# The normed recurrent outputs split into halves during attention, the softmax-merge DMAs on POOL's queue, and the rwkv output weights laid out by block

## The chip, the cores and the metric

The kernel runs on one NeuronCore of a Trainium2 chip. The metric is the device time of one execution in microseconds; the kernel before takes 1726.71 us, the median of 3 runs (1720.41 to 1730.13). The core has a matmul engine (TensorE, PE in the profile; its weight loads are PEld), a vector engine (VectorE, DVE), an activation engine (ScalarE, ACT), GpSimd (POOL) and SyncE (SP). SP computes nothing and issues DMAs; ACT and POOL issue DMAs too, each on a queue of its own, in the order of that engine's instructions. All matrix work on PE runs in a 32-bit form whose products are made exact enough by splitting each factor into a high and a low half (hi, lo) and adding three products, hi·hi, hi·lo and lo·hi. The high half is a rounded copy on ACT, the low half a subtraction on DVE.

## The reference, cut to what matters

```python
h = rms_norm(x, norm1_gain)
p = h @ w_in
q, k, v, p_rwkv, p_gate = jnp.split(p, [...], axis=-1)
...
for g, (win, dil) in enumerate(ATT_PATTERNS):     # 3 groups of 4 heads, dilation 1, 4, 16
    o_g, l_g = dilated_window_attention(q[:, :, g], k[:, :, g], v[:, :, g], ..., win, dil)
...
wts = jax.nn.softmax(jnp.stack(lses, axis=0), axis=0)          # over the 3 groups
att = jnp.einsum('gbsh,gbshe->bshe', wts, jnp.stack(outs, axis=0))
y_att = att.reshape(B, S, ATT_OUT_WIDTH) @ w_att_out           # 256 -> 1024
y_rwkv = rwkv7_time_mix(p_rwkv, ...)                           # ends in o @ w_rwkv_out, 512 -> 1024
gates = jax.nn.sigmoid(p_gate)
mixed = gates[..., :D] * y_att + gates[..., D:] * y_rwkv
x = x + mixed @ w_out
x = x + hierarchical_moe(rms_norm(x, norm2_gain), ...)         # 32 experts, top 2 of a group
```

S = 1024 tokens, D = 1024, everything in fp32.

## The kernel before, in words

Activations lie transposed: a tile holds 128 channels on the partitions and the 1024 tokens along the free axis. The program runs, in this order: the input projection, its gate columns being kept as filler work; the rwkv chunk scan, whose normed outputs go to a DRAM scratch dON (4 tiles of 128 x 1024); attention; a mixing stage; the out-projection with the router; and the 32 experts.

**Attention** runs six units (3 groups x 2 pairs of heads) of eight blocks each. Between the blocks, `fill` emits matmuls of the gate columns; their tanh goes to the scratch dGA from POOL's queue, 128 x 512 at a time. At the end of a unit, `finish` writes the unnormalized output Og to the scratch dOG and the row maxima and sums to dML.

**The mixing stage** is what the change edits. Before, it does the following.

- It loads dON, splits it into ohi and olo (line 1111 for the loads, 1087 and 1088 for the hi and lo half of every `split`), and loads the eight small tiles MLc from dML, from ACT's queue (line 1116).
- From MLc it makes the weights of the softmax over the three groups (wgt, lines 1118 to 1127), stores them to dWG (ACT's queue, line 1129), and reads them back later as broadcasts over 64 partitions (wb, named raw<-dWG, ACT's queue, line 1192).
- The rwkv projection: for eight blocks n of 128 output channels and two halves h of the tokens, 12 matmuls (`mm3`, line 1096) into one PSUM tile pa, of which there are three. The weight block wr comes from SP (line 1137) and is split into wrh and wrl. DVE multiplies the result with the gate and stores it in mix (line 1178). At the same time the blocks of w_out are loaded (line 1182) and split into woh and wol, 16 pairs of 128 x 512.
- The merge: for each of the two pairs of heads, three dOG tiles are multiplied with their broadcasts (line 1193, the third on POOL) and added (1197); the sum is split into ahi and alo.
- The attention projection: w_att_out has two blocks (line 1204), each split into hi and lo; 16 PSUM tiles of 6 matmuls; DVE multiplies with the gate (1219), and DVE or POOL adds to mix (1220).
- The out-projection starts with the splits of mix by 128 tokens (mxh), made in the pool pmx.

**What sets the order.** The kernel is written with a tile framework: every engine gets its own list of instructions, and a scheduler puts them in order by the order of the code and by priorities (`high_priority`; a negative offset defers). A tile pool hands out buffers; a tile whose buffer was used before waits for the last reader of the earlier one. A pool that is opened after another was closed may take its memory, and then its first writer waits for the readers of what lay there. An engine runs its list strictly in order, so a DMA that an engine issues waits in that list like any other instruction. DMAs also share a small set of completion semaphores in turn, so that an issue can wait for an earlier transfer on the same semaphore. In the mixing stage all this is decided by the scheduler.

**The junction** to the out-projection: ACT's list holds six small DMA issues there (lines 1345 to 1361: a gain row, the router's weights and biases, constants rc, and a zero fill of an output strip, zpad). In the expert weights' prefetch, SP loads the first expert matrices into tiles that come free (line 1326).

Of the kernel before, what the change touches and what calls it, by code (L numbers as in the profile page):

```python
# [34 lines left out]
NRAW2 = 5  # L35
# [76 lines left out]
def host_layout(inp):  # L112
# [70 lines left out]
def block_kernel(ctx, tc, I, out, dbg=None):  # L183
# [697 lines left out]

    s3 = ExitStack()
# [34 lines left out]
    def prelude(u):  # L917
# [46 lines left out]
        u.Og = p4.tile([128, S], F32, name="Og")  # L964
# [115 lines left out]
    s9 = ctx.enter_context(ExitStack())  # L1080
    mr = s9.enter_context(tc.tile_pool(name="mr", bufs=NRAW, reuse_waits="tile"))
# [3 lines left out]

    def split(hi, lo, raw):
        nc.scalar.activation(hi, raw, AF.Copy)
        nc.vector.tensor_tensor(lo, raw, hi.bitcast(F32), op=ALU.subtract)
# [11 lines left out]
    pmx = s9.enter_context(tc.tile_pool(name="pmx", bufs=2, reuse_waits="tile"))  # L1100
    s6 = ExitStack()
    pf = s6.enter_context(tc.tile_pool(name="pf", bufs=1, reuse_waits="tile"))
    ohi = pf.tile([128, 4, S], F32R, name="ohi")
    olo = pf.tile([128, 4, S], F32R, name="olo")
    ahi = pf.tile([128, 2, S], F32R, name="ahi")
    alo = pf.tile([128, 2, S], F32R, name="alo")
    s7 = ExitStack()
    p7 = s7.enter_context(tc.tile_pool(name="p7", bufs=2, reuse_waits="tile"))
    for p in range(4):
        raw = raw4k()  # L1110
        nc.sync.dma_start(raw, dON[p])
        split(ohi[:, p], olo[:, p], raw)
    ML = p7.tile([128, 2, 3, 32], F32, name="MLc", bufs=1)
    for a in range(2):
        for h in range(4):
            nc.scalar.dma_start(ML[32 * h:32 * h + 32, a], dML[a, h].rearrange("g (b t) -> b g t", t=32))
    mm_ = p7.tile([128, 32], F32, name="mmin", bufs=1)
    nc.vector.tensor_tensor(mm_, ML[:, 0, 0], ML[:, 0, 1], op=ALU.min)
    nc.vector.tensor_tensor(mm_, mm_, ML[:, 0, 2], op=ALU.min)
    wg = p7.tile([128, 3, 32], F32, name="wgt", bufs=1)  # L1120
# [4 lines left out]
    nc.vector.tensor_tensor(mm_, mm_, ML[:, 1, 2], op=ALU.add)
    nc.vector.reciprocal(mm_, mm_)
    nc.vector.tensor_tensor(wg, wg, mm_[:, None, :].to_broadcast([128, 3, 32]), op=ALU.mult)
    for h in range(4):
        nc.scalar.dma_start(dWG[h].rearrange("g (b t) -> b g t", t=32), wg[32 * h:32 * h + 32])

    wav = I["w_att_out"].rearrange("(k p) n -> p k n", p=128)
    wrv = I["w_rwkv_out"].rearrange("(k p) n -> p k n", p=128)
    wrs = {}

    def load_wr(n):
        wr = p7.tile([128, 4, 128], F32, name="wr")
        nc.sync.dma_start(wr, wrv[:, :, 128 * n:128 * n + 128])
# [5 lines left out]
    load_wr(0)  # L1143
    load_wr(1)
# [562 lines left out]
```

## Time and profile before

| | |
|---|---|
| median of 3 runs | 1726.71 us (1720.41 to 1730.13) |
| profiled execution | 1720.78 us |
| its span in the profile | 1719.0 us |
| mean granted TensorE clock | 0.981 |
| PE busy | 1644.6 us, 96% of the span |
| DVE busy | 1194.2 us |
| ACT busy | 871.3 us |
| POOL busy | 287.3 us |
| DMA traffic | 363.44 MB, mean 211 GB/s |

The stages in the trace of that execution, in us from the start of the span: attention to about 890, its last gate matmul at 899; the rwkv projection from 904 to 961; the attention projection from 962 to 987; the out-projection and the router to 1104; the experts to the end. A row of a timeline has the start, the duration, the engine, the line, the operation, output and inputs, shapes and how many were merged, and in brackets the idle time of the engine just before it and what ended it. PE's matmuls overlap, so the distance of two starts is the pace, not the duration of a row. PEclk is the granted clock as a share of full speed. The DMA share is the mean busy share of the core's 16 DMA engines.

### The profile page before, as it was taken

What the parts mean: (1) busy time and instruction counts of PE and PEld (TensorE: products, weight loads), DVE (VectorE), ACT (ScalarE), POOL (GpSimd) and SP (SyncE); (2) the same over time, 40 slices, a digit from 0 to 9 for tenths busy, and PEclk for the clock granted to TensorE, in tenths of its full rate; (3) what the DMA queues carried; (4) which work ended last, traced back from release to release, by engine and by line L of the source; (5) the groups of instructions that cost most, each with busy time, mean ns of one, the idle gap of its engine ahead of it and who ended that gap; (6) DMA issues with size and microseconds to landing.
All of it is one profiled execution on the core that took longest, in us unless ns stands there. A gap on an engine that the chain in (4) does not pass through costs nothing. (4 is left out here: it accounts for less than half of the span.)

```text
span 1719.0 us, 25855 instructions
## 1 busy us (share of the span) xinstructions
PE 1644.6 (96%) x9395; PEld 1308.6 (76%) x9396; DVE 1194.2 (69%) x2181; ACT 871.3 (51%) x1315; POOL 287.3 (17%) x314
## 2 busy tenths in 40 slices
PE   8999998999999999999998899789999999999996
PEld 6677777777777777777766677678888888888884
DVE  5648798784552444434336756689999999998985
ACT  4524444423221333344343122378888888887774
POOL 0100103133430000000100221212221222211211
PEclk9999999999999999999998999889999999999998
DMA  8324324476642111111249783679999999999994
GB/s 297 130 80 137 116 87 153 141 239 195 210 138 73 37 44 37 45 41 53 88 149 269 213 298 134 239 255 376 382 374 365 375 371 374 363 363 354 373 373 119
DMA packets 145619, 363.44 MB, mean 211 GB/s; under 512 B 17316, under 2 KB 62772, under 8 KB 145484
## 3 DMA queue, kind: packets, MB, share of 16 engines
q1 hardware_dynamic: 123108, 303.67, 49.1%
q0 software_dynamic: 15872, 50.35, 10.5%
q10 hardware_dynamic: 6504, 7.69, 1.7%
q8 instruction: 76, 1.25, 0.3%
q14 instruction: 59, 0.48, 0.1%
HBM read 307.49 MB, written 62.29 MB: 215 GB/s over the span
## 5 line engine op out<-in xcount | busy, mean ns | idle before, releaser
L1536 PE MATMUL pb<-u,xTh 128*128 128x512 f32 x1024 | 338.2, 406 | 0.5 <-ACT xTh L1531 0.5
L307 PE MATMUL pa<-xhi,wh 128*128 128x512 f32 x736 | 300.3, 408 | 2.9 <-DVE qT L905 1.4
L307 PE MATMUL pa<-xlo,wh 128*128 128x512 f32 x736 | 302.0, 410 | 0.0
L307 PE MATMUL pa<-xhi,wl 128*128 128x512 f32 x736 | 298.2, 406 | 2.4 <-DVE wl L278 2.4
L1422 DVE TENSOR_TENSOR u<-raw,u 128x1024 fp32r<-128x1024 f32 x216 | 254.7, 1219 | 18.0 <-ACT u L1421 15.9
L1421 ACT ACTIVATE u<-raw 128x1024 fp32r<-128x1024 f32 x216 | 223.6, 1056 | 30.6 <-PE pb L1536 19.0
L1536 PEld LDWEIGHTS pb<-u,xTh 128*128 128x128 f32 x1024 | 191.1, 189 | 40.3 <-ACT xTh L1531 1.2
L1536 PE MATMUL pb<-u,xTl 128*128 128x512 f32 x512 | 207.5, 405 | 0.0
L307 PEld LDWEIGHTS pa<-xhi,wh 128*128 128x128 f32 x736 | 140.3, 191 | 35.9 <-DVE qT L905 1.7
L307 PEld LDWEIGHTS pa<-xhi,wl 128*128 128x128 f32 x736 | 140.3, 191 | 34.9 <-DVE wl L278 3.2
L307 PEld LDWEIGHTS pa<-xlo,wh 128*128 128x128 f32 x736 | 140.4, 191 | 34.6 <-issue 4.0
L1422 DVE TENSOR_TENSOR u<-mix,u 128x1024 fp32r<-128x1024 f32 x128 | 151.4, 1219 | 11.2 <-ACT u L1421 10.0
L1536 PE MATMUL pa<-u,hTh 128*128 128x512 f32 x512 | 143.4, 401 | 0.9 <-ACT hTh L1531 0.9
L1421 ACT ACTIVATE u<-mix 128x1024 fp32r<-128x1024 f32 x128 | 133.2, 1057 | 16.6 <-PE pb L1536 9.6
L980 DVE SCALAR_TENSOR_TENSOR Sb<-pb,rqk,bias 128x128 f32<-128x128 f32 (+1 forms) x96 | 35.5, 408 | 126.7 <-PE pb L979 119.0
L1515 POOL DMA_INDIRECT out<-row,tba x30 | 78.8, 2628 | 202.1 <-ACT u L1421 171.5
L1536 PEld LDWEIGHTS pa<-u,hTh 128*128 128x128 f32 x512 | 93.5, 188 | 22.4 <-ACT hTh L1531 1.5
L1536 PEld LDWEIGHTS pb<-u,xTl 128*128 128x128 f32 x512 | 96.8, 189 | 17.6 <-DVE xTl L1532 0.2
L276 ACT ACTIVATE wh<-wr 128x1024 fp32r<-128x1024 f32 x49 | 51.8, 1056 | 107.3 <-PE pa L307 88.6
L1536 PE MATMUL pa<-u,hTl 128*128 128x512 f32 x256 | 80.7, 396 | 1.2 <-DVE hTl L1532 1.2
L1509 POOL DMA_INDIRECT xin<-dH,tbl x32 | 38.2, 1194 | 250.8 <-PE pb L1530 248.0
L984 ACT ACTIVATE Sb<-Sb,ML 128x128 f32<-128x128 f32 (+1 forms) x96 | 42.3, 442 | 54.5 <-DVE ML L982 54.5
(415 smaller groups left out, 2823.8 us busy)
## 6 DMA issues: line engine op xcount, KB each, us to landing
raw<-in_w_expert_up SPq DMA_DIRECT2D x72, 512.0 KB, 11.8
raw<-in_w_expert_gate SPq DMA_DIRECT2D x71, 512.0 KB, 5.3
raw<-in_w_expert_down SPq DMA_DIRECT2D x71, 512.0 KB, 12.2
wr<-in_w_in SPq DMA_DIRECT2D x49, 512.0 KB, 3.5
mix<-in_w_expert_down SPq DMA_DIRECT2D x46, 512.0 KB, 13.0
mix<-in_w_expert_gate SPq DMA_DIRECT2D x42, 512.0 KB, 5.0
mix<-in_w_expert_up SPq DMA_DIRECT2D x40, 512.0 KB, 11.9
dGA<-gs POOLq DMA_DIRECT2D x32, 256.0 KB, 2.9
```

The lines of the kernel that those rows point to most:

```text
L276: nc.scalar.activation(wh, wr, AF.Copy)
L307: nc.tensor.matmul(ps, a[:, k, :], b[:, k, hs], start=(n == 0), stop=(n == 23))
L980: nc.vector.scalar_tensor_tensor(Sb[:, hh, 0:nk], pS[:, 0:nk], u.rn[:, 0, i, hh:hh + 1], u.bias[:, hh, 256 - nk:], op0=ALU.mult, op1=ALU.add)
L984: nc.scalar.activation(Sb[:, hh, 0:nk], Sb[:, hh, 0:nk], AF.Exp, bias=u.ML[:, i, hh:hh + 1], accum_out=u.ML[:, i, 2 + hh:3 + hh])
L1421: nc.scalar.activation(hi, raw, AF.Copy)
L1422: nc.vector.tensor_tensor(lo, raw, hi.bitcast(F32), op=ALU.subtract)
L1509: nc.gpsimd.indirect_dma_start(out=dst, out_offset=None, in_=src, in_offset=bass.IndirectOffsetOnAxis(ap=idx, axis=0), bounds_check=S - 1, ...
L1515: nc.gpsimd.indirect_dma_start(out=out, out_offset=bass.IndirectOffsetOnAxis(ap=idx, axis=0), in_=src, in_offset=None, compute_op=ALU.add)
L1536: nc.tensor.matmul(ps, x, w, start=first, stop=last)
```

## The change

1. The halves ohi and olo get eight tiles of their own in a pool `pf` that is opened before attention. A generator `on_steps` loads dON from POOL's queue and splits it, one step per attention block, from the second unit on. For the room, Og goes from two buffers to one, Sb from three to two, and mt takes a slot that other tiles of attention share.
2. The last unit's writes to dOG and dML go out on POOL's queue, and so do the loads of MLc, the stores of dWG, the loads of dOG and the broadcasts wb. The third product of the merge moves from POOL to DVE. The steps that make the weights are a generator that is advanced inside the loop over n, the last two of them with a negative priority offset.
3. w_rwkv_out is laid out on the host as 8 blocks, so that a load of a block reads 2 KB runs; the first two loads get priority. Gates are loaded as full rows (128 x 1024) instead of halves.
4. The eight slots of `pf` serve afterwards as gate tiles (fs), as places for the expert prefetch and for the low halves of the first two splits of mix. Raw tiles `mr` and the pool of ahi and alo close with the mixing stage, and pmx is opened after that.

```diff
+    s9 = ctx.enter_context(ExitStack())
+    pf = s9.enter_context(tc.tile_pool(name="pf", bufs=1, reuse_waits="tile"))
+    ohi = [pf.tile([128, S], F32R, name=f"ohi{p}") for p in range(4)]
+    olo = [pf.tile([128, S], F32R, name=f"olo{p}") for p in range(4)]
...
+    def on_steps():
+        for p in range(4):
+            yield
+            raw = p4.tile([128, S], F32, tag="sq", name="raw")
+            nc.gpsimd.dma_start(raw, dON[p])
+            yield
+            split(ohi[p], olo[p], raw)
...
-        u.Og = p4.tile([128, S], F32, name="Og")
+        u.Og = p4.tile([128, S], F32, name="Og", bufs=1)
...
-        Sb = p4.tile([128, 2, 256], F32, name="Sb", bufs=3)
+        Sb = p4.tile([128, 2, 256], F32, name="Sb", bufs=2)
...
-        nc.sync.dma_start(dOG[2 * u.g + u.hp], u.Og)
+        q = nc.gpsimd if u is units[-1] else nc.sync
+        q.dma_start(dOG[2 * u.g + u.hp], u.Og)
         for hh in range(2):
-            nc.sync.dma_start(dML[:, 2 * u.hp + hh, u.g], mt[hh:4:2])
+            q.dma_start(dML[:, 2 * u.hp + hh, u.g], mt[hh:4:2])
...
             fill(FA)
+            if n > 0:
+                next(ons, None)
...
-    pmx = s9.enter_context(tc.tile_pool(name="pmx", bufs=2, reuse_waits="tile"))
-    s6 = ExitStack()
...
-            nc.scalar.dma_start(ML[32 * h:32 * h + 32, a], dML[a, h].rearrange("g (b t) -> b g t", t=32))
+                nc.gpsimd.dma_start(ML[32 * h:32 * h + 32, a], dML[a, h].rearrange("g (b t) -> b g t", t=32))
...
-        nc.scalar.dma_start(dWG[h].rearrange("g (b t) -> b g t", t=32), wg[32 * h:32 * h + 32])
+            nc.gpsimd.dma_start(dWG[h].rearrange("g (b t) -> b g t", t=32), wg[32 * h:32 * h + 32])
...
-        nc.sync.dma_start(wr, wrv[:, :, 128 * n:128 * n + 128])
+        nc.sync.dma_start(wr, I["w_rwkv_out"][n])
...
-    load_wr(0)
-    load_wr(1)
+    with tc.high_priority(offset=600):
+        load_wr(0)
+        load_wr(1)
...
+        if n in (0, 2, 3):
+            with tc.high_priority(offset=-400 if n else 0):
+                next(mw, None)
...
-            nc.sync.dma_start(og, dOG[2 * g + hp])
+            nc.gpsimd.dma_start(og, dOG[2 * g + hp])
             wb = raw4k()
             for hh in range(2):
-                nc.scalar.dma_start(wb[hrs[hh]], dWG[2 * hp + hh, g:g + 1].to_broadcast([64, S]))
-            (nc.gpsimd if g == 2 else nc.vector).tensor_tensor(og, og, wb, op=ALU.mult)
+                nc.gpsimd.dma_start(wb[hrs[hh]], dWG[2 * hp + hh, g:g + 1].to_broadcast([64, S]))
+            nc.vector.tensor_tensor(og, og, wb, op=ALU.mult)
...
     s7.close()
     s6.close()
+    pmx = s9.enter_context(tc.tile_pool(name="pmx", bufs=2, reuse_waits="tile"))
...
-            ml = raw4k().bitcast(F32R).rearrange("q (n t) -> q n t", t=128)
+            ml = fslot(7 - i).bitcast(F32R).rearrange("q (n t) -> q n t", t=128)
```

The order of instructions moves at three places that matter below. A row has the line, the operation, output and inputs, the shape, and how many follow one another. The first place is ACT's list from the end of the last attention unit (Og, mt) into the rwkv projection. Before:

```order
L1012 ACTIVATE Og<-pb 128x8x64
L1026 ACTIVATE mt<-pb 4x8x64 x2
L383 ACTIVATE gs<-gs 128x512
L1087 ACTIVATE ohi<-raw 128x1024 x4
L1116 DMA MLc<-dML 32x3x32 x8
L1087 ACTIVATE wrh<-wr 128x512
L1122 ACTIVATE wgt<-wgt 128x96
L1087 ACTIVATE wrh<-wr 128x512
```

With the change:

```order
L1035 ACTIVATE Og<-pb 128x8x64
L1049 ACTIVATE mt<-pb 4x8x64 x2
L385 ACTIVATE gs<-gs 128x512
L894 ACTIVATE wrh<-wr 128x512
L385 ACTIVATE gs<-gs 128x512
L894 ACTIVATE wrh<-wr 128x512
L1139 ACTIVATE wgt<-wgt 128x96
```

The four copies ohi and the eight loads MLc no longer stand between the last evacuations of attention and the first wrh.

The second place is POOL's list from the last unit's writes to the last broadcast. Before, POOL had the dGA stores, two products of the merge and additions to mix there, and no load. With the change:

```order
L1054 DMA dOG<-Og 128x1024
L1056 DMA dML<-mt 2x1024 x2
L386 DMA dGA<-gs 128x512
L1132 DMA MLc<-dML 32x3x32 x8
L386 DMA dGA<-gs 128x512
L1214 DMA raw<-dOG 128x1024
L1147 DMA dWG<-wgt 32x3x32 x4
L1217 DMA raw<-dWG 64x1024 x2
L1214 DMA raw<-dOG 128x1024
L1217 DMA raw<-dWG 64x1024 x2
```

The pair of the last two rows comes six times in all. All of the merge's transfers now stand in one list.

The third place is ACT's list at the junction to the out-projection. Before:

```order
L1087 ACTIVATE raw<-raw 128x1024
L1087 ACTIVATE mxh<-mix 128x1024 x2
L1345 DMA g_8582<-in_g 128x1024
L1347 DMA wr_8584<-in_w_rt 128x8x36
L1349 DMA g2c<-in_g2c 128x8
L1352 DMA br_8589<-in_b_rt 128x36
L1354 DMA rc<-in_rc 128x208
L1361 DMA out<-zpad 1024x1x128
L1472 ACTIVATE pa,ss_8620<-xt 128x512
```

With the change:

```order
L894 ACTIVATE raw<-raw 128x1024
L1368 DMA g_8572<-in_g 128x1024
L1370 DMA wr_8574<-in_w_rt 128x8x36
L1372 DMA g2c<-in_g2c 128x8
L1375 DMA br_8579<-in_b_rt 128x36
L1377 DMA rc<-in_rc 128x208
L1384 DMA out<-zpad 1024x1x128
L894 ACTIVATE mxh<-mix 128x1024 x2
L1495 ACTIVATE pa,ss_8606<-xt 128x512
```

The copies mxh have moved behind the six DMA issues.

More of the change, by code (lines that the diff above doesn't have):

```diff
@@ L34 @@
 NRAW = 6
-NRAW2 = 5
+NRAW2 = 3
+NS8 = 8
 BHT = 2
@@ L143, in host_layout @@
     f["bucket1h"], f["relmask"] = host_bucket()
-    for k in ("w_att_out", "w_rwkv_out", "w_out"):
+    for k in ("w_att_out", "w_out"):
         f[k] = inp[k][0]
+    f["w_rwkv_out"] = inp["w_rwkv_out"][0].reshape(4, 128, 8, 128).transpose(2, 1, 0, 3)
     f["g2c"] = inp["norm2_gain"][0].reshape(8, 128).T
@@ L879, in block_kernel, with fslot, split @@
     sT.close()
+    s9 = ctx.enter_context(ExitStack())
+    pf = s9.enter_context(tc.tile_pool(name="pf", bufs=1, reuse_waits="tile"))
+    ohi = [pf.tile([128, S], F32R, name=f"ohi{p}") for p in range(4)]
+    olo = [pf.tile([128, S], F32R, name=f"olo{p}") for p in range(4)]
+    ftags = [f"ohi{p}" for p in range(4)] + [f"olo{p}" for p in range(4)]
+    def fslot(j):
+        return pf.tile([128, S], F32, tag=ftags[j], name="fs")
+    def split(hi, lo, raw):
+        nc.scalar.activation(hi, raw, AF.Copy)
+        nc.vector.tensor_tensor(lo, raw, hi.bitcast(F32), op=ALU.subtract)
+    def on_steps():
[5 more added lines that the diff above has]
+            split(ohi[p], olo[p], raw)
     s3 = ExitStack()
@@ L1097, in mm3 @@
                 i += 1
-    pmx = s9.enter_context(tc.tile_pool(name="pmx", bufs=2, reuse_waits="tile"))
-    s6 = ExitStack()
[L1102 to L1106, printed above, removed]
+    pa_ = s6.enter_context(tc.tile_pool(name="pa_", bufs=1, reuse_waits="tile"))
+    ahi = pa_.tile([128, 2, S], F32R, name="ahi")
@@ L1107, in block_kernel @@
+    alo = pa_.tile([128, 2, S], F32R, name="alo")
     s7 = ExitStack()
     p7 = s7.enter_context(tc.tile_pool(name="p7", bufs=2, reuse_waits="tile"))
[L1109 to L1114, printed above, removed]
-        for h in range(4):
-            nc.scalar.dma_start(ML[32 * h:32 * h + 32, a], dML[a, h].rearrange("g (b t) -> b g t", t=32))
@@ L1170, in block_kernel @@
     wov = I["w_out"].rearrange("(k p) n -> p k n", p=128)
+    mw = merge_weights()
+    ga1 = gate(1, 0)
     for n in range(8):
         wh, wl = wrs.pop(n)
+        ga = ga1
+        if n + 1 < 8:
+            ga1 = gate(1, n + 1)
         for h in range(2):
             hs = slice(512 * h, 512 * h + 512)
-            ga = gate(1, n, h)
             ps = psA.tile([128, 512], F32, name="pa")
-            mm3(ps, [((wh[:, k], wl[:, k]), (ohi[:, k, hs], olo[:, k, hs])) for k in range(4)])
-            nc.vector.scalar_tensor_tensor(mixv(n, h), q4(ga), 1.0, q4(ps), op0=ALU.add, op1=ALU.mult)
+            mm3(ps, [((wh[:, k], wl[:, k]), (ohi[k][:, hs], olo[k][:, hs])) for k in range(4)])
+            nc.vector.scalar_tensor_tensor(mixv(n, h), q4(ga[:, hs]), 1.0, q4(ps), op0=ALU.add, op1=ALU.mult)
         if n + 2 < 8:
@@ L1206, in block_kernel @@
         split(wa[k][0], wa[k][1], raw[k])
-    gas = []
-    for tag in ("ohi", "olo"):
-        t = pf.tile([128, 8, 512], F32, tag=tag, name=tag + "g")
-        gas += [t[:, j] for j in range(8)]
+    gas = [gate(0, n) for n in range(2)]
+    gas += [gate(0, 2 + j, fslot(j)) for j in range(6)]
     for h in range(2):
@@ L1292, in block_kernel @@
     mr2 = s9.enter_context(tc.tile_pool(name="mr2", bufs=NRAW2, reuse_waits="tile"))
[L1293 removed]
+    areas = ["mr2"] * NRAW2 + [("s", j) for j in range(NS8)] + list(range(8)) + ["mx"] * 2 + ["ph"] * NPH
     NR = len(areas)
@@ L1461, in block_kernel @@
             if c == 1 and i < 7:
-                load_raw(N0 + NRAW2 + NRAW + i)
+                load_raw(N0 + NRAW2 + NS8 + i)
                 load_x(i + 1)
                 if i == 1:
-                    for j in range(NRAW):
+                    for j in range(NS8):
                         load_raw(N0 + NRAW2 + j)
```

56 lines of the change are left out of this document (28 added, 28 removed).

## The prediction, made before the result was known

> **What bounds the kernel now.** I read the page first, then the waits of TensorE, then the windows around those waits, and only then the timelines of PE, ACT and SP in them.
>
> ```profile
> span 1719.0 us, 25855 instructions
> PE 1644.6 (96%) x9395; PEld 1308.6 (76%) x9396; DVE 1194.2 (69%) x2181; ACT 871.3 (51%) x1315; POOL 287.3 (17%) x314
> ```
>
> PE works for 96% of the span. The change adds and removes no matmul, so it can only touch the 74 us in which PE is idle, and the stretches in which its clock is low. Everything it edits lies between the second attention unit and the first router matmul, so I cut the trace there (columns: window, its length, then busy time of PE, PEld, DVE, ACT and POOL, granted clock, DMA share, GB/s).
>
> ```profile
> 880.00:899.50 19.50, 19.50 (x92) 14.73 (x92) 6.09 (x9) 9.62 (x15) 1.63 (x3) 1.00 0.39 133
> 899.50:904.00 4.50, 0.05 (x2) 0.04 (x1) 2.30 (x4) 0.63 (x1) 0.00 (x0) 0.90 1.01 381
> 904.00:961.90 57.90, 51.01 (x192) 39.60 (x192) 36.89 (x57) 16.75 (x28) 5.32 (x3) 0.89 0.92 255
> 961.90:987.20 25.30, 24.15 (x97) 19.02 (x98) 20.96 (x29) 3.08 (x3) 10.25 (x7) 0.93 0.64 209
> 987.20:1050.00 62.80, 62.69 (x324) 50.35 (x323) 38.23 (x170) 16.30 (x42) 12.68 (x17) 1.00 0.72 256
> ```
>
> Attention's end is clean, then PE stands still for 4.5 us while the DMA engines are full, the rwkv projection (192 matmuls) and the attention projection (96) run with gaps and at clocks 0.89 and 0.93, and from 987.2 on PE is full again. The timeline of PE shows each gap, and what a gap does to the clock.
>
> ```profile
> 899.12 0.39 PE L307 MATMUL pa<-xhi,wl 128*128 128x512 f32 x1
> 903.96 0.80 PE L1096 MATMUL pa<-ohi,wrh 128*128 128x512 f32 x1 [4.45 <-ACT wrh L1087]
> 909.19 0.63 PE L1096 MATMUL pa<-ohi,wrl 128*128 128x512 f32 x1
> 910.22 0.39 PE L1096 MATMUL pa<-ohi,wrl 128*128 128x512 f32 x1
> 933.82 0.39 PE L1096 MATMUL pa<-olo,wrh 128*128 128x512 f32 x1
> 935.78 0.47 PE L1096 MATMUL pa<-ohi,wrh 128*128 128x512 f32 x1 [1.35 <-DVE mix L1178]
> 937.42 0.80 PE L1096 MATMUL pa<-ohi,wrl 128*128 128x512 f32 x1 [0.94 <-DVE wrl L1088]
> 947.32 0.69 PE L1096 MATMUL pa<-ohi,wrl 128*128 128x512 f32 x1 [2.64 <-DVE wrl L1088]
> 961.94 0.47 PE L1096 MATMUL pa<-ahi,raw 128*128 128x512 f32 x1 [1.55 <-DVE mix L1178]
> 964.72 1.22 PE L1096 MATMUL pa<-ahi,raw 128*128 128x512 f32 x2 [0.57 <-DVE raw L1088]
> ```
>
> Between the rows at 910.22 and 933.82 lie 104 matmul steps, 0.227 us each: that is the full pace. After the 4.45 us gap it is 0.43 us until 909.2, so thirteen matmuls lose 0.2 us each, 2.6 us. 288 matmuls at full pace are 65.4 us; from 899.5 to 987.2 they took 87.7. So **22 us** is all that can be won here; about half is idle, the rest slow clock and waiting for PSUM.
>
> Who is late is read from ACT and SP.
>
> ```profile
> 900.20 3.04 ACTq L1116 DMA_DIRECT2D MLc<-dML  x5
> 903.28 0.63 ACT L1087 ACTIVATE wrh<-wr 128x512 fp32r<-128x512 f32 x1 [4.14 <-DMA MLc<-dML]
> 907.42 1.82 ACTq L1129 DMA_DIRECT2D dWG<-wgt  x4
> 941.85 0.63 ACT L1087 ACTIVATE wrh<-wr 128x512 fp32r<-128x512 f32 x1 [10.06 <-DMA raw<-dWG]
> 950.87 0.63 ACT L1087 ACTIVATE wrh<-wr 128x512 fp32r<-128x512 f32 x1 [7.25 <-DMA raw<-dWG]
> 962.30 1.06 ACT L1087 ACTIVATE raw<-raw 128x1024 fp32r<-128x1024 f32 x1 [1.15 <-DMA raw<-in_w_att_out]
> 978.38 2.02 ACT L1087 ACTIVATE mxh<-mix 128x1024 fp32r<-128x1024 f32 x2 [15.02 <-POOL mix L1220]
> 987.42 0.35 ACTq L1345 DMA_DIRECT2D g<-in_g  x1
> 990.88 0.34 ACTq L1354 DMA_DIRECT2D rc<-in_rc  x1
> 992.23 0.64 ACTq L1361 DMA_DIRECT2D out<-zpad  x1
> ```
>
> ACT's weight splits (wrh) stand in line behind DMAs that ACT issues itself (MLc, then the broadcasts raw<-dWG), each of which waits for something: 4.14, 10.06 and 7.25 us. PE waits for what hangs on those splits.
>
> **The change, part by part.**
>
> *The first stall.* Before, SP issued the first rwkv weight block behind the loads of dON and w_out:
>
> ```profile
> 894.99 0.93 SPq L1137 DMA_DIRECT2D wr<-in_w_rwkv_out  x2
> 948.43 0.33 SPq L1204 DMA_DIRECT2D raw<-in_w_att_out  x1
> 958.83 0.33 SPq L1204 DMA_DIRECT2D raw<-in_w_att_out  x1
> 986.46 0.34 SPq L1326 DMA_DIRECT2D raw<-in_w_expert_up  x1
> 986.90 0.38 SPq L1326 DMA_DIRECT2D raw<-in_w_expert_gate  x1
> ```
>
> Now the blocks stand ahead of the last unit's outputs, which leave SP for POOL, and MLc is no longer on ACT, so wrh can be split as soon as ACT has done the last attention evacuations (about 896). wrl is a DVE step behind the last gate product, about 901. I put the first gap at 0.6 us without a clock loss: 4.45 + 2.6 - 0.6 = 6.4 us won, if nothing later takes it. Bounds: 0 (the gap stays) and 7.
>
> *The halves in attention* cost four ACT copies and four DVE subtractions of 128x1024, which is what the rows of these forms cost in the expert stage:
>
> ```profile
> L1422 DVE TENSOR_TENSOR u<-raw,u 128x1024 fp32r<-128x1024 f32 x216 | 254.7, 1219 | 18.0 <-ACT u L1421 15.9
> L1421 ACT ACTIVATE u<-raw 128x1024 fp32r<-128x1024 f32 x216 | 223.6, 1056 | 30.6 <-PE pb L1536 19.0
> ```
>
> That is 4.2 us of ACT and 4.9 us of DVE, moved from 895-900 into attention's second unit, where gate matmuls fill PE. I take 0.7 us, between 0 and 4 (one such pair in the way of a softmax step each time: half of 9.1). Og with one buffer, Sb with two, and mt in a shared slot wait for readers of a block earlier; I count them in that 0 to 4.
>
> *The rwkv stage.* 192 x 0.227 = 43.7 us from 900.1: it ends at about 943.8 (961.9 before), if DVE, which evacuates the three PSUM tiles, isn't held. DVE does hold broadcast products in its order, and these wait for wb; a second place for a stall of 0 to 5 us (before: 1.35 + 0.94 + 2.64), 0 taken, because what follows waits anyway.
>
> *The merge and the attention projection.* POOL now issues 2 dML, 8 MLc, 4 dWG, 6 dOG and 12 wb loads. Its price of an issue:
>
> ```profile
> L384 POOL DMA_DIRECT2D dGA<-gs x12 | 6.6, 547 | 92.0 <-ACT gs L383 92.0
> ```
>
> 32 x 0.55 = 17.6 us of POOL, which is otherwise idle here; ACT loses its waits. But wgt's last product is pushed down (priority -400) behind six rwkv evacuations, 900.1 + 6 x 2.73 = 916.5 plus DVE's queue, about 919, where dWG went out at 907.42 before. The dWG stores then end at about 921.5. Three dOG tiles and three broadcasts, 3 MB, take 12 us at the window's 255 GB/s; three products, two sums and two halves of about 1.2 us each, 8.4, follow, a little of them beneath the loads: the first half-pair is done near 941. Its wb loads are followed by the second half-pair's, whose last one waits for the first alo (raw slots), so near 945 for the last wb.
>
> What ends the wait is the second w_att_out block. Before, from its issue at 958.83 through landing, the ACT half (962.30) and the DVE half to PE's row at 964.72 took 5.9 us. It now waits for the lo half of the first block; the first block is queued on SP behind a gate load that needs the fifteenth rwkv product (about 941.8) and lands with 2 MB of gates in front of it (8 us at that rate), about 949.5; hi 1.06 and lo 1.22 make 951.8. So the second goes out at 952 and PE is released at **952 + 5.9 = 958**, against 964.7. Bounds: 952 (the first block isn't behind the gates' bytes) and 963 (it lands as late as before).
>
> PE has 15 of the 96 matmuls behind it by then (three tiles of five), so the projection ends at 958 + 81 x 0.227 + 2.3 (slow clock and a late PSUM, as after 964.72) = **978.7**, against 987.2: **8.5 us** won. The rwkv stage's gain beyond that becomes waiting between 944 and 958.
>
> *The junction.* In before the splits of mix for the out-projection (mxh) ran at 978.38, 9 us ahead of need, and ACT's six DMA issues came after them. Now pmx is opened after the pools of this stage close, so mxh waits for the last attention matmul, and in ACT's order it stands behind the six. Three of these take semaphores on which expert loads have to land: before, rc went out 4.4 us after the up load's issue, and zpad 5.3 us after the gate load's (986.46 to 990.88, 986.90 to 992.23). Now the last load goes out when the mix addition for n=5 frees its slot, about when the projection ends (T). So: T + 4.3 to 5.3 for zpad, + 0.64 for its issue, + 1.04 for mxh, and 0.6 until the low half serves: PE idle 6.6 to 7.6 us, plus 2.6 us of slow clock as after the gap at 899.5. I take **9 us lost**, 6.5 to 12. Before, the loss here was 0.1 us (62.69 of 62.80). What would hide it, matmuls that don't need mix, isn't there: PE's order goes straight on.
>
> A rule of the Trainium skill (TensorE: Matmul & The Clock Gate, Part 1) says the clock falls to half after an idle window of about 3.4 us. The trace goes further: it fell after 2.64 us too, and after 1.35 + 0.94. By either, the two new waits (944 to 958, and the junction) each bring one warm-up.
>
> *The rest.* Row order by block makes 2 KB runs of w_rwkv_out instead of 512 B, full-row gates 4 KB instead of 2 KB: earlier landings, contained in the times above. The expert prefetch has 23 slots in both. Router and experts shift one to one with T.
>
> **Sum**, against the profiled execution (1720.78 us, span 1719.0): -8.5 + 9 + 0.7 = +1.2, 1722. This execution lies 5.9 us below the median of the three (1726.71, from 1720.41). A like median would be 1727.9; I take 1726, since three runs don't fix a median to 2 us.
>
> **Rivals.**
>
> 1. *The junction is cheaper or the weights come sooner: faster.* If the second w_att_out block is in by 952, T = 952 + 18.4 + 2.3 = 972.7 (-14.5), and with loads that land in 3.5 us (the block issued at 958.83 was in at 962.30) the junction is 6: -8.5 + 0.7 on that side, 1713 for the profiled execution, 1718 for the median. For it: the DMA share in 961.9 to 987.2 is only 0.64. Against: wgt is later by 12 us.
> 2. *The junction is dear: slower.* It decides when the loads in front of rc and zpad need more than about 11 us:
>
> ```profile
> raw<-in_w_expert_up SPq DMA_DIRECT2D x72, 512.0 KB, 11.8
> ```
>
> With 11.8 in place of 5.3 the loss is 9 + 6.5 = 15.5: -8.5 + 15.5 + 0.7 = +7.7, and with W at 961 in place of 958 it is +10.7, so 1732 to 1737. Against it: that is the figure of a full queue, and at 986 it was 4.4.
> 3. *The queue move does nothing.* The same bytes at DMA share 0.92 set the merge, whichever queue issues them, and the projection's wait ends at 964.7 as now: 964.7 + 20.7 = 985.4, -1.8 + 9 + 0.7 = +7.9, 1729 to 1734. For it: the share. Against: ACT's 4.14, 10.06 and 7.25 us were spent in line, not on bytes. The Trainium skill (DMA: Bandwidth & Descriptors, "Issuing engines are not separate DMA queues") speaks for this rival: DMAs of all issuing engines run on the same 16 DMA engines, so another queue saves issue time alone.
>
> **How the numbers follow.** A measurement of this kernel can tell about 0.5%, 8.6 us. Forecast 0.48, rival 1 0.25, rival 2 0.13, rival 3 0.14, of which a little under half comes out over the bound. So faster 0.25, same 0.56, slower 0.19. The range: forecast with its bounds (W -6 to +5, junction -2.5 to +3, attention -0.7 to +3.3, ends not all together) is 1718 to 1735; stretched to most of rivals 1 and 3 and of 2, 1713 to 1737.
>
> **What would show it.** Right: no wait on MLc at ACT, a first rwkv matmul before 901, rwkv at 0.227 us a matmul, a PE wait on a w_att_out half (raw) that ends between 952 and 963, and one on mxh of 5 to 8 us just behind the last attention-projection matmul, with ACT's rc and zpad issues in front of mxh. Wrong: waits on wrl or mix inside rwkv (DVE held by broadcasts), no wait on mxh, gaps within attention, or a shift in the expert stage that isn't that of T.

## The result: 1.1% slower, and the profile after

The changed kernel takes 1740.3 us, the median of 8 runs (1737.04 to 1750.02), the kernel before 1721.08 us, the median of 8 (1717.28 to 1734.46). The ratio is **1.0112, 95% interval 1.0094 to 1.0131**. The forecast was 1726, no change, in a range from 1713 to 1737: it was wrong. Two executions of the runs below, one of 2021.52 us with the early slot and one of 3182.84 us with all four repairs, were in a slow state and are left out of the medians.

The page of the changed kernel, its span and the engines:

```profile
span 1738.1 us, 25873 instructions
PE 1644.9 (95%) x9395; PEld 1310.3 (75%) x9396; DVE 1197.1 (69%) x2183; ACT 871.0 (50%) x1315; POOL 308.3 (18%) x349
```

PE is busy for as long as before (1644.6 us then); 18.8 of the 19.1 us of the longer span are time in which PE stands still, before or after its last matmul. The waits of PE, the new ones on top:

```profile
PE pa L1119 <- ACT raw L894: 17.5, 2, 16.3
PE pa L1119 <- ACT mxh L894: 8.6, 1, 8.6
...
PE pa L1119 <- DVE fs L895: 2.3, 1, 2.3
...
PE pa L1119 <- DVE wrl L895: 0.5, 1, 0.5
```

The 4.45 us on wrh are gone, and of the 4.0 us on wrl 0.5 are left. In their place stand one wait of 16.3 us on a half of w_att_out and one of 8.6 us on mxh. The windows, cut at the ends of the stages (columns as in the prediction):

```profile
900.50:945.00 44.50, 43.97 (x193) 35.74 (x191) 31.71 (x52) 14.25 (x26) 11.18 (x21) 1.00 0.79 244
945.00:961.30 16.30, 0.05 (x1) 0.00 (x0) 6.00 (x6) 1.43 (x2) 2.62 (x5) 0.56 0.96 308
961.30:989.30 28.00, 26.63 (x96) 20.03 (x96) 21.19 (x28) 2.11 (x2) 9.99 (x9) 0.83 0.30 98
989.30:1004.50 15.20, 4.21 (x9) 2.91 (x10) 3.75 (x8) 2.00 (x2) 1.38 (x4) 0.57 1.00 354
```

The rwkv projection (first row) now runs at full clock with a single gap of 0.53 us, in 44.5 us where it took about 61 with its first stall. Then PE stands for 16.3 us with the DMA engines at 0.96, and after the attention projection once more for most of 15.2 us, with the DMA engines at 1.00. The timeline of PE at these two places and at its end:

```profile
902.07 0.50 PE L1119 MATMUL pa<-ohi,wrl 128*128 128x512 f32 x1 [0.53 <-DVE wrl L895]
...
944.66 0.39 PE L1119 MATMUL pa<-ohi,wrl 128*128 128x512 f32 x1
961.34 0.79 PE L1119 MATMUL pa<-ahi,raw 128*128 128x512 f32 x1 [16.29 <-ACT raw L894]
...
967.17 0.80 PE L1119 MATMUL pa<-ahi,raw 128*128 128x512 f32 x1 [1.22 <-ACT raw L894]
...
997.95 0.80 PE L1119 MATMUL pa<-woh,mxh 128*128 128x512 f32 x1 [8.65 <-ACT mxh L894]
...
1001.51 0.79 PE L1119 MATMUL pa<-woh,fs 128*128 128x512 f32 x1 [2.34 <-DVE fs L895]
...
1721.32 0.63 PE L1559 MATMUL pa<-u,hTl 128*128 128x512 f32 x2
```

Who is late is again read from SP, ACT and DVE, one fence each:

```profile
948.99 0.32 SPq L1181 DMA_DIRECT2D ga<-dGA  x1
949.48 0.33 SPq L1229 DMA_DIRECT2D raw<-in_w_att_out  x1
962.58 0.33 SPq L1229 DMA_DIRECT2D raw<-in_w_att_out  x1
988.71 0.33 SPq L1349 DMA_DIRECT2D fs<-in_w_expert_gate  x1
```

```profile
960.23 1.06 ACT L894 ACTIVATE raw<-raw 128x1024 fp32r<-128x1024 f32 x1 [14.86 <-DMA raw<-in_w_att_out]
...
990.27 1.46 ACTq L1372 DMA_DIRECT2D g2c<-in_g2c  x1
...
993.93 1.11 ACTq L1377 DMA_DIRECT2D rc<-in_rc  x1
996.10 0.63 ACTq L1384 DMA_DIRECT2D out<-zpad  x1
996.84 2.00 ACT L894 ACTIVATE mxh<-mix 128x1024 fp32r<-128x1024 f32 x2 [29.72 <-DMA g<-in_g]
```

```profile
961.32 1.23 DVE L895 TENSOR_TENSOR raw<-raw 128x1024 fp32r<-128x1024 f32 x1 [5.31 <-ACT raw L894]
962.46 1.22 DVE L1218 TENSOR_TENSOR raw<-raw 128x1024 f32<-128x1024 f32 x1
...
967.21 1.22 DVE L895 TENSOR_TENSOR raw<-raw 128x1024 fp32r<-128x1024 f32 x1
...
999.86 0.46 DVE L1373 TENSOR_TENSOR wr<-wr,g2c 128x288 f32<-128x288 f32 x1 [9.54 <-DMA g2c<-in_g2c]
1000.24 2.35 DVE L895 TENSOR_TENSOR fs<-mix,mxh 128x1024 fp32r<-128x1024 f32 x2
```

The first w_att_out block was issued at 949.48 and was in at 960.2, 10.7 us later. At the junction the expert load whose semaphore zpad shares went out at 988.71, zpad's issue waited until 996.10, and mxh (996.84) stood behind it, as forecast. What was not forecast: its low half (1000.24) stands on DVE behind the product with g2c, and g2c, issued at 990.27, was in only at 999.86.

**Where the 19.1 us are.** I cut every run at the starts of four matmuls: A, the last gate matmul; T, the last of the attention projection; R, the last of the out-projection; M, the last row of all (two matmuls). (In us; each entry is the difference of two starts in the timeline of PE, from one profiled execution; the third column is the last rwkv matmul after A.)

| kernel | A | rwkv end after A | A to T | T to R | R to M | M to the end | span |
|---|---|---|---|---|---|---|---|
| before | 899.1 | 60.9 | 87.8 | 117.1 | 601.7 | 13.3 | 1719.0 |
| changed | 900.2 | 44.4 | 88.7 | 130.9 | 601.5 | 16.8 | 1738.1 |
| difference | +1.1 | -16.5 | +0.9 | **+13.8** | -0.2 | **+3.5** | +19.1 |

The rwkv projection's 16.5 us were given back in full before the attention projection ended. The junction cost 13.8, and the end of the program 3.5.

### The profile page after: what moved, and what is told of

It reads as the page before. It is cut to its first block, busy times and chain, and to the rows that moved or that the text cites. A ratio compares the mean times of both kernels' runs of the same rounds, so it can differ in the third digit from the quotient of the medians.

```text
span 1738.1 us, 25873 instructions
## 1 busy us (share of the span) xinstructions
PE 1644.9 (95%) x9395; PEld 1310.3 (75%) x9396; DVE 1197.1 (69%) x2183; ACT 871.0 (50%) x1315; POOL 308.3 (18%) x349
## 5 line engine op out<-in xcount | busy, mean ns | idle before, releaser
L1445 DVE TENSOR_TENSOR u<-fs,u 128x1024 fp32r<-128x1024 f32 x133 | 157.5, 1221 | 8.9 <-ACT u L1444 6.2
L1444 ACT ACTIVATE u<-fs 128x1024 fp32r<-128x1024 f32 x133 | 137.7, 1057 | 18.0 <-PE pb L1559 10.8
L1444 ACT ACTIVATE u<-mix 128x1024 fp32r<-128x1024 f32 x128 | 133.2, 1057 | 16.5 <-PE pb L1559 8.6
L1445 DVE TENSOR_TENSOR u<-raw,u 128x1024 fp32r<-128x1024 f32 x83 | 98.4, 1221 | 7.7 <-ACT u L1444 6.6
L278 ACT ACTIVATE wh<-wr 128x1024 fp32r<-128x1024 f32 x49 | 51.8, 1056 | 94.2 <-PE pa L309 74.3
L1444 ACT ACTIVATE u<-raw 128x1024 fp32r<-128x1024 f32 x83 | 86.3, 1056 | 11.5 <-PE pb L1559 6.4
```

Source lines behind the costliest of these rows:

```text
L278: nc.scalar.activation(wh, wr, AF.Copy)
```

## The experiments

Theories, when the runs were written. For the junction: "line", mxh stands behind issues on ACT and its low half behind a product on DVE, against "late memory". For the attention projection: something late in the queue of transfers (gates in front of the weights or broadcasts), against "bytes", full DMA engines whatever the order.

| run | median, us | ratio to before, 95% | A to T | T to R | M to the end |
|---|---|---|---|---|---|
| junction issues on POOL | 1728.18 | 1.0041 (1.0025 to 1.0057) | 89.8 | 119.1 | 17.1 |
| early slot for the first split | 1736.15 | 1.0108 (1.0067 to 1.0149) | 89.4 | 125.0 | 16.5 |
| w_att_out early | 1741.92 | 1.0104 (1.0083 to 1.0125) | 93.1 | 130.7 | 16.5 |
| early slot and w_att_out early | 1732.55 | 1.0064 (1.0044 to 1.0084) | 88.2 | 125.4 | 16.6 |
| junction and gates on POOL | 1734.6 | 1.0061 (1.0027 to 1.0095) | 89.3 | 119.2 | 18.0 |
| junction on POOL, no deferral | 1724.09 | 1.0011 (0.9986 to 1.0036) | 87.7 | 119.4 | 17.1 |
| merge back on ACT and SP | 1742.02 | 1.0132 (1.0097 to 1.0167) | 90.2 | 131.4 | 13.8 |
| all four repairs | 1720.34 | 0.9983 (0.9962 to 1.0005) | 74.8 | 119.5 | 17.9 |
| junction on SP, w_att_out early, no deferral | 1717.38 | 0.997 (0.995 to 0.9989) | 80.2 | 120.6 | 16.8 |
| halves after attention | 1744.81 | 1.0125 (1.0074 to 1.0175) | 93.1 | 131.1 | 17.0 |
| old layout of w_rwkv_out | 1744.19 | 1.0115 (1.007 to 1.0161) | 90.1 | 130.5 | 16.6 |
| before, 40 more POOL transfers | 1730.24 (one run) | | 87.9 | 117.6 | 16.6 |

The kernel before had medians from 1721.67 to 1722.02 beside these runs. A lies between 896.4 and 907.2 in them, for a reason told at the end, so that single spans mislead and the stages are compared. A stage of one execution has a spread too: between A and T the engines' lists of the third and the fourth run are the same but for a few rows near T, and A to T is 93.1 and 88.2 us, 3.4 of these 4.9 us in the rwkv projection (48.6 and 45.2). A difference of up to 5 us in A to T between two single executions is therefore no evidence by itself.

**1. The junction's issues on POOL.**

```diff
-    nc.scalar.dma_start(g2, I["g2"].to_broadcast([128, S]))
+    nc.gpsimd.dma_start(g2, I["g2"].to_broadcast([128, S]))
...
-    nc.scalar.dma_start(out[S:S + 128].rearrange("q (j c) -> q j c", j=8), zpad[:, None, :].to_broadcast([128, 8, 128]))
+    nc.gpsimd.dma_start(out[S:S + 128].rearrange("q (j c) -> q j c", j=8), zpad[:, None, :].to_broadcast([128, 8, 128]))
```

(the four between them likewise)

> The six DMA issues at the junction (gain row, router weights and biases, constants, zero strip) go out on POOL's queue instead of ACT's; pmx still opens after the mixing stage closes, so mxh still waits for the last attention matmul. Theory 'line' (mxh was late because it stood on ACT behind issues that wait for expert loads, and its low half stood on DVE behind a product that waits for one of those transfers): mxh starts within 0.5 us of the last attention matmul, PE idles about 2 to 2.5 us there, loses some slow clock, 3.5 us in all instead of 13.9: total about 10 us under the changed kernel, near 1730. Rival 'late memory' (the wait is for the memory of the closed pools, the line costs nothing): mxh still starts 7 to 8 us after the last matmul, total unchanged near 1740.

1728.18 us, and T to R 119.1 instead of 130.9. The timeline of PE in this run, the last matmul of the attention projection and the first waits of the out-projection:

```profile
986.22 0.39 PE L1120 MATMUL pa<-ahi,raw 128*128 128x512 f32 x1
987.82 0.50 PE L1120 MATMUL pa<-woh,mxh 128*128 128x512 f32 x1 [1.21 <-ACT mxh L895]
...
989.84 0.50 PE L1120 MATMUL pa<-woh,fs 128*128 128x512 f32 x1 [0.34 <-DVE fs L896]
```

1.55 us of waits are left of 10.99 (8.65 and 2.34). pmx's memory was freed as late as before, so "late memory" falls: the line cost 11.8 of the 13.8 us. In this run the scheduler also put the low half ahead of the product with g2c on DVE, so the run undoes both lines at once.

**2. A slot that is free early, for the first split.** ACT's issues stay where they are.

```diff
-        mh = pmx.tile([128, 8, 128], F32R, name="mxh")
-        if i < 2:
+        if i == 0:
+            mh = fslot(6).bitcast(F32R).rearrange("q (n t) -> q n t", t=128)
+        else:
+            mh = pmx.tile([128, 8, 128], F32R, name="mxh")
+        if i < 1:
             ml = fslot(7 - i).bitcast(F32R).rearrange("q (n t) -> q n t", t=128)
```

> The high half of the first mix split gets a slot of pf (the one of olo2), which is free since the rwkv projection, instead of a pmx buffer; ACT's issues stay on ACT. Both theories of the junction ('line' and 'late memory'): the first split is done before the attention projection ends, PE loses under 1 us there, about 13 to 14 us less than the changed kernel: 1726. If the junction's loss comes from elsewhere (expert loads that take the DMA engines from the out-projection's own inputs), the total falls by less than 5 us.

Missed: 1736.15 us instead of 1726. Its three executions lie between 1733.69 and 1746.36, so that a gain over the changed kernel can't be told, though T to R fell by 5.9 us in the profile. ACT, DVE and PE of this run:

```profile
980.96 1.07 ACT L894 ACTIVATE fs<-mix 128x1024 fp32r<-128x1024 f32 x1 [11.94 <-POOL mix L1242]
```

```profile
1000.82 0.46 DVE L1373 TENSOR_TENSOR wr<-wr,g2c 128x288 f32<-128x288 f32 x1 [9.76 <-DMA g2c<-in_g2c]
1001.19 0.68 DVE L1493 SCALAR_TENSOR_TENSOR xt<-pa,xt 128x512 f32<-128x512 f32 x1
1001.79 1.22 DVE L895 TENSOR_TENSOR mxl<-mix,mxh 128x1024 fp32r<-128x1024 f32 x1
```

```profile
1001.93 0.66 PE L1410 MATMUL pb<-ident,xt 128*128 128x128 f32 x4 [1.02 <-DVE xt L1493]
1005.88 0.69 PE L1410 MATMUL pb<-ident,xt 128*128 128x128 f32 x2 [2.83 <-DVE xt L1493]
```

The first split starts at 980.96, 8 us ahead of need. But DVE waits 9.76 us for g2c and only then evacuates the first results (L1493) and makes the second low half, and PE waits for the evacuations (1.02 and 2.83 us). The junction is two lines, on ACT and on DVE; taking one away leaves about half.

**3. The w_att_out blocks early**, in a pool of their own (8 KB a partition), **and 4. both repairs so far together.**

```diff
+    pwa = s6.enter_context(tc.tile_pool(name="pwa", bufs=2, reuse_waits="tile"))
...
+        if n == 2:
+            raw = [pwa.tile([128, S], F32, name="waw") for k in range(2)]
+            for k in range(2):
+                nc.sync.dma_start(raw[k], wav[:, k])
...
-    raw = [raw4k(), raw4k()]
     wa = []
     for k in range(2):
-        nc.sync.dma_start(raw[k], wav[:, k])
```

> The two w_att_out blocks get two tiles of their own (8 KB a partition) and are loaded in the middle of the rwkv projection; nothing else is changed against the changed kernel. Theory 'behind the gates' (the blocks landed late because they queue on SP behind gate loads and 4 MB of gates and broadcasts were in front of them): their halves are ready near 945 to 950 us, DVE isn't held by a missing block between the merge's products, the second pair's alo ends near 959 to 960 and PE is released there instead of 968.4; the attention projection ends near 980 instead of 989: total 8 to 9 us under the changed kernel, near 1731. Rival 'bytes' (the DMA engines are full from 925 to 965 and the same bytes pass in any order): the last broadcasts come later by what the blocks took, PE is released at 965 to 968, total at most 3 us lower.

> The early slot for the first mix split and the early w_att_out blocks together. If 'behind the gates' and the junction's theories hold, the gains add: 13 + 9 = 22 us under the changed kernel, near 1718, a little under the kernel before (1721). With 'bytes' only the junction's part comes: near 1726.

"Behind the gates" missed: A to T is 93.1 and 88.2 us, against 88.7 in the changed kernel; the medians are 1741.92 and 1732.55 us, where 1731 and 1718 were expected. With the weights in, the last broadcasts hold PE. POOL's and DVE's timelines in the run with both:

```profile
946.50 1.04 POOL L1222 DMA_DIRECT2D raw<-dWG  x2
```

```profile
960.89 1.23 DVE L1223 TENSOR_TENSOR raw<-raw 128x1024 f32<-128x1024 f32 x1 [3.51 <-DMA raw<-dWG]
```

The last broadcast was issued at about 947 and in at 960.9, 14 us later. In the changed kernel that product ran at 962.46, held on DVE behind the late w_att_out half: the broadcast had landed at 959.6, the w_att_out block at 960.2. Two transfers end at about the same time, and which of them is blamed depends on the order on DVE.

**5. The gates of the attention projection on POOL's queue**, behind the last broadcast, on top of run 1.

```diff
-    gas = [gate(0, n) for n in range(2)]
-    gas += [gate(0, 2 + j, fslot(j)) for j in range(6)]
+    gas = [gate(0, n, q=nc.gpsimd) for n in range(2)]
+    gas += [gate(0, 2 + j, fslot(j), q=nc.gpsimd) for j in range(6)]
```

> On top of the run with the junction's issues on POOL: the eight full-row gate loads of the attention projection (4 MB) go out on POOL's queue, behind the last broadcast, instead of SP's. Theory 'gates before broadcasts' (the second pair of heads is late because its last broadcasts and the w_att_out blocks share full DMA engines with gates that aren't needed yet): the last broadcast lands within 6 us of its issue instead of 14, the second pair's alo is ready near 955 to 957 after a rwkv start at 896, and the time from the last gate matmul to the end of the attention projection falls from 90 to 82 to 84 us: total near 1721. Rival 'bytes': the gates, now later, hold the evacuations of the attention projection instead, PE waits on those, and the total stays at 1727 to 1730.

A to T 89.3 against 89.8 in run 1: nothing won, and the median is not lower but higher (1734.6 against 1728.18). The gates went out right behind the last broadcast, which landed 9.3 us after its issue (expected: within 6), and the w_att_out blocks, still late, shared the engines with them.

**6. No deferral of the merge weights**, on top of run 1.

```diff
-            with tc.high_priority(offset=-400 if n else 0):
+            with tc.high_priority(offset=0):
```

> On top of the run with the junction's issues on POOL: the negative priority of the merge weights is taken away, so that the last product of wgt stands on DVE behind three rwkv evacuations instead of six. Theory 'late weights' (the broadcasts start 10 us later than need be, while the DMA engines are half idle from 915 to 925): dWG goes out near 910 instead of 920, both pairs end 6 to 8 us earlier, total near 1721. Rival 'bytes': the broadcasts only queue earlier, the merge's end moves by less than 2 us, total 1726 to 1729.

1724.09 us, 4 us under run 1 (half of what was expected), A to T 2.1 us less in the profile. The merge did start earlier, but DVE now met its products inside the rwkv projection before their broadcasts had landed, and PE paid there (DVE, then PE):

```profile
927.22 1.22 DVE L1218 TENSOR_TENSOR raw<-raw 128x1024 f32<-128x1024 f32 x1 [5.43 <-DMA raw<-dWG]
935.48 1.23 DVE L1218 TENSOR_TENSOR raw<-raw 128x1024 f32<-128x1024 f32 x1 [4.11 <-DMA raw<-dWG]
```

```profile
938.62 0.79 PE L1119 MATMUL pa<-ohi,wrh 128*128 128x512 f32 x1 [3.80 <-DVE mix L1200]
957.47 0.79 PE L1119 MATMUL pa<-ahi,raw 128*128 128x512 f32 x1 [7.85 <-ACT raw L894]
```

The rwkv projection ends 51.8 us after A instead of 45.2, and then the weights are still late (7.85).

**7. The merge's transfers back on ACT and SP**, otherwise the changed kernel.

```diff
-                nc.gpsimd.dma_start(ML[32 * h:32 * h + 32, a], dML[a, h].rearrange("g (b t) -> b g t", t=32))
+                nc.scalar.dma_start(ML[32 * h:32 * h + 32, a], dML[a, h].rearrange("g (b t) -> b g t", t=32))
...
-            nc.gpsimd.dma_start(dWG[h].rearrange("g (b t) -> b g t", t=32), wg[32 * h:32 * h + 32])
+            nc.scalar.dma_start(dWG[h].rearrange("g (b t) -> b g t", t=32), wg[32 * h:32 * h + 32])
...
-            nc.gpsimd.dma_start(og, dOG[2 * g + hp])
+            nc.sync.dma_start(og, dOG[2 * g + hp])
...
-                nc.gpsimd.dma_start(wb[hrs[hh]], dWG[2 * hp + hh, g:g + 1].to_broadcast([64, S]))
+                nc.scalar.dma_start(wb[hrs[hh]], dWG[2 * hp + hh, g:g + 1].to_broadcast([64, S]))
```

(and the last unit's writes on SP)

> The changed kernel with only the queues undone: last unit's writes and dOG loads on SP, MLc, dWG and broadcasts on ACT. Theory 'the merge sets the release of PE': ACT's weight splits wait in line again and PE waits on wrl by 3 to 9 us inside the rwkv projection, but the attention projection still ends within 3 us of the changed kernel's (989, a little later at most); the junction's loss (13.9 us) stays, since mxh stays behind the issues: total 1737 to 1744. If the 3.4 us that the changed kernel needs more between its last matmul and its end come from the larger number of transfers issued on POOL, they vanish here (13.3 instead of 16.8); if not, they stay. Rival 'the queue was the cost': total back at 1721 to 1727.

1742.02 us: the queue was not the cost. ACT waits in line again (5.20 us for MLc ahead of wrh), the rwkv projection ends 49.3 us after A instead of 44.4, and A to T is 90.2 against 88.7. So the move to POOL took these waits out of the rwkv projection (4.9 us in these two executions), and no gain from it is shown in A to T (1.5 us, inside the spread). The waits of PE inside the projection were smaller than expected (1.72 and 0.94 us, not 3 to 9). The time after the last matmul fell back to 13.8.

**8. All four repairs, and 9. without the gates' queue** (junction issues on SP, w_att_out early, no deferral).

> Junction issues on POOL, attention gates on POOL behind the broadcasts, merge weights not deferred, and w_att_out blocks loaded early into tiles of their own. If each of the causes is real, the gap between the rwkv and the attention projection shrinks to a few us, the stage from the last gate matmul to the end of the attention projection takes 70 to 76 us (87.7 before, 89 with the change, 65.4 at full pace), and the total is near 1710 to 1714, under the kernel before (1721). With 'bytes' the stage stays over 82 us and the total at 1719 or more.

> The changed kernel with three repairs: the six junction issues on SP's queue, w_att_out loaded early into tiles of its own, merge weights not deferred; the attention gates stay on SP. The run with all repairs had 74.8 us from the last gate matmul to the end of the attention projection, while each repair alone left 88 to 93. Theory 'two lines end together' (the weights and the merge each hold PE until about the same moment, so that only both together move it; the gates' queue doesn't matter): 74 to 78 us here too, out-projection and router 117 to 120, total near 1712 to 1716. Rival 'all three are needed': over 82 us and 1720 or more.

With all four, A to T is 74.8 us: 13.9 less than in the changed kernel, where the w_att_out repair alone won nothing and the deferral and the gates' queue, each on top of run 1, won 2.1 and 0.5. The stage came out as expected (70 to 76), the total didn't: 1720.34 us instead of 1710 to 1714. PE's timeline in the run with all four, between the two projections:

```profile
944.71 0.47 PE L1119 MATMUL pa<-ahi,raw 128*128 128x512 f32 x1 [1.37 <-DVE mix L1201]
946.89 1.10 PE L1119 MATMUL pa<-ahi,raw 128*128 128x512 f32 x2 [1.48 <-DVE raw L895]
949.22 0.79 PE L1119 MATMUL pa<-ahi,raw 128*128 128x512 f32 x1 [0.60 <-DVE mix L1201]
951.44 1.65 PE L1119 MATMUL pa<-ahi,raw 128*128 128x512 f32 x3 [0.58 <-ACT ahi L894]
```

The 16.3 us gap has become four of 0.6 to 1.5 us. Without the gates' queue the stage is 80.2 us, between the two theories' numbers. That the gates' queue matters is not shown: 4.1 of the 5.4 us lie in the rwkv projection (45.0 and 49.1 us after A), the profiled execution is the fastest of run 8 (1712.88) and the slowest of run 9 (1722.58), and the medians go the other way. Run 9's, 1717.38 us over 12 runs, with a ratio of 0.997 (0.995 to 0.9989), is the only one under the kernel before by more than its interval. It lies 10.8 us under run 1, which has the junction's repair alone; no deferral brought 4.1 of that on its own, and the early w_att_out blocks on their own brought nothing (1741.92 against 1740.3).

**10. The halves made after attention, 11. the old layout**, each undone alone in the changed kernel.

```diff
-            if n > 0:
-                next(ons, None)
...
     finish(units[-1])
+    for _ in ons:
+        pass
```

```diff
-        nc.sync.dma_start(wr, I["w_rwkv_out"][n])
+        nc.sync.dma_start(wr, I["w_rwkv_out"].rearrange("(k p) n -> p k n", p=128)[:, :, 128 * n:128 * n + 128])
```

> The changed kernel with the loads and splits of the recurrent outputs moved behind the last attention unit; everything else stays. Theory 'the merge sets the release of PE': the rwkv projection starts 3 to 6 us later, but the attention projection ends within 3 us of the changed kernel's 88.7 us after the last gate matmul, total 1738 to 1744: the first stall's removal was worth nothing here. Rival 'the halves in attention cost': attention gets faster by 1 us or more and the total falls to 1736 or lower.

> The changed kernel with w_rwkv_out in its old layout, loaded in runs of 512 B. Both theories: no step of PE hangs on these loads now, so each stage within 1 us of the changed kernel, total 1737 to 1743. If the layout had been a cost or a gain by itself, the total moves by more than 4 us.

Without the halves in attention PE waits 15.93 us for the first wrh (expected: a start 3 to 6 us later), the rwkv projection ends 24.3 us later after A (68.7), and A to T rises by 4.4 us (expected: within 3). So of the 24 us that the halves in attention won at most 4.4 were left at T, no more than two executions of nearly the same lists differ by. A itself, 901.5, lies inside the spread of A, so that no cost within attention shows. The layout moved the stages by at most 1.4 us (expected: within 1), about as much as A to T differs among runs that share that part (88.7, 89.8, 89.4): nothing shown for or against it.

**12. More transfers on POOL, in the kernel before.**

```diff
+    dz = p4.tile([1, 40, 8], F32, name="dz", bufs=1)
+    for j in range(40):
+        nc.gpsimd.dma_start(dz[:, j], I["rc"][0:1, 64:72])
     finish(units[-1])
```

> The kernel before with 40 added loads of 32 bytes on POOL's queue at the start of attention, nothing else. The time from the last matmul to the end was 13.3 us in the kernel before, 13.8 with the merge back on other queues (4 more POOL transfers), 16.8 in the changed kernel (37 more), 17.9 to 18.0 with 51 more. Theory 'each transfer issued on POOL costs 0.09 us at the end of the program': 13.3 + 40 x 0.09 = 16.9 us here. Rival 'it is something else in the changed kernel': 13.3 us.

16.6 us from the last matmul to the end, against 13.3. PE's last row and POOL's last row, first in the kernel before, then in this run:

```profile
1705.74 0.63 PE L1536 MATMUL pa<-u,hTl 128*128 128x512 f32 x2
```

```profile
1707.75 1.42 POOL L1515 DMA_INDIRECT out<-xin,tba  x1 [15.66 <-ACTq L1667]
```

```profile
1711.91 0.63 PE L1539 MATMUL pa<-u,hTl 128*128 128x512 f32 x2
```

```profile
1713.92 1.42 POOL L1518 DMA_INDIRECT out<-xin,tba  x1 [15.65 <-ACTq L1670]
```

POOL's last scatter starts 2.0 us after PE's last row in both; all of the difference lies behind it. 3.3 us for 40 transfers are 0.08 us each; the changed kernel's 37 more would be 3.1 of its 3.5. That the program's end takes longer when POOL has issued more transfers, here about 1200 us earlier (from 533 us on) and 32 bytes each, is shown; what the end does with them is not.

## Why the prediction was wrong, point by point

- **The first stall** and the rwkv projection: right. The first gap was 0.53 us (0.6 forecast), the end 944.7 (943.8), the clock full.
- **The release of PE for the attention projection** is the step that failed: "952 + 5.9 = 958". The 5.9 us held (962.58 to 968.4); the term that was mis-sized is the landing of the first w_att_out block, "about 949.5". It landed at 960.2, 10.7 us later than that. The forecast had it issued behind a gate load at 941.8, with 8 us of gates in front of it. But SP's list, in order, held a gate load that went out only at 948.99, when DVE had finished the last rwkv product, so that the block was issued at 949.48 (7.7 us of the 10.7); then gates and the broadcasts for the second pair shared the engines, and it took 10.7 us to land (the other 3). The second block could go only after the low half of the first (961.32 and 1.23 on DVE), at 962.58, and PE had it all at 968.4 (967.21 and 1.22 on DVE), 5 us beyond the bound of 963. A to T came out at +0.9, not -8.5: that is 9.4 of the 17.9 us between the span and the forecast.
- The repair of that one term would not have saved the step: runs 3, 4 and 6 show the weights and the broadcasts each within a few us of holding PE. The forecast made a chain with one last link where there were several of the same length. Rival 3 ("the same bytes") described the stage better than the forecast: by run 7, another issuing engine gave ACT its 5 us of waits in line back and moved A to T by 1.5 us only. That agrees with its rule from the Trainium skill (DMA: Bandwidth & Descriptors, "Issuing engines are not separate DMA queues"), by which another queue saves issue time alone. Yet not only the bytes bound: in an order in which they start earlier, the same bytes pass in a stage of 74.8 us in run 8 and 80.2 in run 9.
- **The junction**: the mechanism was right (rc and zpad in front of mxh, PE idle just behind the last attention matmul), the size 13.8 instead of 9, beyond the bound of 12. About half remains when mxh's line on ACT alone is gone (run 2), through a second line that the forecast had not looked for: DVE's list, with the product that waits for g2c ahead of the low half. The expert load in front of zpad took 7.4 us to let it go (988.71 to 996.10), where 5.3 was taken. Rival 2, which put the whole loss on that landing, had its price about right (15.5) and its cause half right.
- **Halves in attention**: 0.7 us forecast; A moved by 1.1, which can't be told from the spread of A.
- **The router and the experts**: shifted one to one, as forecast (R to M 601.7 and 601.5).
- **The end of the program**: 3.5 us that the forecast did not have at all. POOL was called "otherwise idle", and the 32 new transfers that the forecast counted there (37 with the loads of dON and the write of dOG) were priced at their issue alone.
- Sum: 0.9 + 13.8 + 3.5 + 1.1 - 0.2 = 19.1, where +1.2 was forecast.

## What to carry to other kernels

When a wait is taken away in a stage whose DMA engines are nearly full, list every transfer that the next step needs and when each lands; if several land within a few us, a single repair may show little, and the set of them is worth a run. When a tile moves into memory that is freed late, read all engines' lists at that place, not only the list that the tile's first writer stands on: DMA issues, and products that wait for them, may now be ahead of it. And a queue that looks idle may still send a bill: here at the end of the program.

## What the runs showed of the hardware that was not expected

- Each transfer issued on POOL's queue lengthened the end of the program by about 0.08 us: 13.3 us with 160 of them, 13.8 with 164, 16.8 with 197, 16.6 with 200, 17.9 with 211 (the DMA rows of POOL in the traces).
- The same instructions up to A took 896.4 to 907.2 us. The windows show where: the clock in three stretches with many small gaps, here of run 1 and of run 5:

```profile
100.00:150.00 50.00, 46.79 (x237) 37.17 (x237) 31.41 (x75) 17.16 (x30) 2.71 (x8) 1.00 0.30 97
250.00:300.00 50.00, 44.73 (x473) 35.91 (x473) 41.60 (x109) 21.90 (x40) 13.09 (x20) 1.00 0.41 132
350.00:400.00 50.00, 48.34 (x517) 38.36 (x516) 31.63 (x70) 13.16 (x21) 18.58 (x32) 0.97 0.62 220
```

```profile
100.00:150.00 50.00, 47.82 (x229) 38.47 (x228) 30.71 (x73) 16.88 (x29) 2.51 (x7) 0.93 0.25 77
250.00:300.00 50.00, 46.26 (x456) 37.09 (x454) 41.97 (x106) 20.19 (x36) 13.11 (x20) 0.90 0.36 119
350.00:400.00 50.00, 48.33 (x439) 38.68 (x438) 34.00 (x78) 12.38 (x19) 19.11 (x33) 0.85 0.65 216
```

  With the same code, the clock fell in these stretches in one execution (0.93, 0.90, 0.85) and hardly in the other (1.00, 1.00, 0.97). No wait of PE near 250 to 300 was longer than 1.6 us in either. A is 896.4 us in run 1 and 907.2 in run 5, which is the reason to compare stages. Whole executions show the same: of the kernel before, the fastest recorded beside runs 9 to 12 took 1717.2 us at a mean clock of 0.984, the longest 1735.72 at 0.971.
